# One down product for the whole sequence, with a second split in four of its seven products and operand sums made by transfers

## The chip, the cores and the metric

The kernel runs on one core of a Trainium2 chip. The metric is the device time in microseconds (us) of one execution. A core has five engines that run side by side: TensorE (PE) for matmuls, VectorE (DVE) and ScalarE (ACT) for element work, GpSimd (POOL), and SyncE (SP), which here only starts transfers. Each has its own queue of instructions and works through it in order. Sixteen DMA engines carry the transfers of all queues. Matmuls read operands from the on-chip memory SBUF and write to PSUM, eight banks of 128x512 floats each.

## The reference

One decoder layer on x of 2048 positions and 1024 channels, then a last norm: a mixing part (four HGRN2 heads, eight sliding-window attention heads, an output projection) and a gated MLP with a causal depthwise convolution. What matters here is the MLP:

```python
    v = rmsnorm(h, norm_ffn_w[l])
    gate = causal_depthwise_conv(v @ w_gate[l], conv_w[l], conv_b[l])
    h = h + (jax.nn.silu(gate) * (v @ w_up[l])) @ w_down[l]
return rmsnorm(h, final_norm_w)
```

`w_gate` and `w_up` are 1024 x 2816, `w_down` is 2816 x 1024, all float32.

## The kernel before

All activations stand transposed, channels on partitions. The sequence is done in two halves of 1024 positions (`hf` = 0, 1). For each half: the mixing part, the output projection (`out_proj`), the gate and up products (`gate_up`), the down product (`down`). A float32 operand is cut into a high part (`h`, a cast by ACT to the float32r format) and a low part (`l`, the difference, by DVE), and each product of tiles is three matmuls: high x high, high x low, low x high.

The three MLP products use the Winograd form of Strassen's scheme: with both operands split 2 x 2, seven products P1 to P7 stand for eight. In `down` the splits are the 22 k-tiles of 128 channels (even and odd, 11 each), the 8 output tiles (4 and 4) and the 1024 positions (lo and hi, 512 each). The activation operands `B11, T1, B21, T2, T3, B22, T4` are computed by DVE at the end of each pair of `gate_up` and stored to DRAM (`acts`, L1092 to L1105). The weight operands are the four quadrants `A11` to `A22` of `w_down` and the sums `S1` to `S4`, which DVE makes inside `down` (`w_op`, L1125 to L1141). `prep_piece` loads and cuts two k-tiles at a time, two pieces ahead. A product has 4 output tiles, 11 k-tiles and 3 terms: 132 matmuls of 128x512; seven products and two halves make 1848. Sums in PSUM run on from product to product (`bx` on four banks of the pool `mm`, `by` on the banks `hg` and `at`).

`down` of the first half also loads, cuts and sums the squares of the second half's x (`load`, from three pieces before P4 on), so that the key and value units (`first_unit`) and the unit `f` of the second half can follow at once. In the last half the final norm runs beside the last product P4, done column by column (`column`), the last two of them in halves of 256 positions.

`gate_up` goes through 11 pairs of output tiles. Each pair has a gate unit and an up unit (`pair_unit`) of 7 x 12 = 84 matmuls, 1848 in a half. Its weights come through the ring `raw` of three tiles, and its activation operands T2, T3, B22 and T4 lie in the pool `x`, which holds the tiles of x in the mixing part.

The order of instructions on each engine is fixed when the program is built, by a planner that models the time of each instruction and takes from each engine's queue what it expects to be ready first. Instructions of several jobs are put between each other. `tc.issue_after` pins an order. SP issues nearly all transfers, ACT a few small ones; POOL issues none.

Of the kernel before, what the change touches and what calls it, by code (L numbers as in the profile page):

```python
# [17 lines left out]
P = 128  # L18
# [13 lines left out]
PIECES = [2, 2, 2, 2, 2, 1]  # L32
OPS = ["B11", "T1", "B21", "T2", "T3", "B22", "T4"]
QUADS = ["A11", "A12", "A21", "A22"]
PRODUCTS = [("P1", "A11", "B11"), ("P5", "S1", "T1"), ("P6", "S2", "T2"), ("P3", "S4", "B22"),
            ("P7", "S3", "T3"), ("P2", "A12", "B21"), ("P4", "A22", "T4")]
# [17 lines left out]
def hymba_layer(ctx: ExitStack, tc: tile.TileContext, a: dict, out: bass.AP):  # L54
# [8 lines left out]
    xp = pool("x")  # L63
    wp = pool("w")
    hp = pool("h")
    sp = pool("small", bufs=2)
    sp.tile([P, 48], F32, name="pad", bufs=1)
    dp = pool("dram", space=bass.MemoryType.DRAM)
# [758 lines left out]
    def out_proj(hf, M, p):  # L827
# [6 lines left out]
        ops = Operands(p)  # L834
        ops.get("B11", 0)
        kept, v = {}, {}
# [4 lines left out]
        for d, part in parts:  # L841
# [18 lines left out]
            k = kept[d] = dp.tile([P, HALF], F32, name=f"keep{hf}{d}")  # L860
# [3 lines left out]
            for b, bs in halves():  # L864
# [8 lines left out]
                nc.sync.dma_start(k[:, bs], t[:, bs])  # L873
# [36 lines left out]
        return kept, ops, st, first, leftovers  # L910
# [48 lines left out]
    def pair_unit(W, ops, p, evac, then={}, behind_first=None):  # L959
# [35 lines left out]
        if behind_first:  # L995
# [13 lines left out]
            return  # L1009
        prod(X, "S2", "T2", True)  # L1010
        u2 = out(X, "u2")
        Y = ps("hg", "Y")
        prod(Y, "S1", "T1")
        s5 = out(Y, "s5")
# [8 lines left out]
    def gate_up(hf, ops, hs, nxt, last, p):  # L1023

        acts = {op: [dp.tile([P, n, 512], F32, name=f"act{hf}{op}{i}") for i, n in enumerate(PIECES)] for op in OPS}
# [7 lines left out]
        for pr in range(FT // 2):  # L1033
# [21 lines left out]
            if pr == 0:  # L1055
# [5 lines left out]
                pair_unit(W, ops, p, gate, then, behind_first)  # L1061
# [5 lines left out]
            for i in range(2):  # L1067
# [9 lines left out]
                nc.vector.tensor_tensor(y, y, invb, op=ALU.mult)  # L1077
# [12 lines left out]
            pair_unit(W, ops, p, up)  # L1090

            y1, y2 = ys  # L1092
            dst = {op: acts[op][pr // 2][:, pr % 2] for op in OPS}
            tt = slot("T13")
            nc.sync.dma_start(dst["B11"], y1[:, lo])
            nc.sync.dma_start(dst["B21"], y2[:, lo])
            nc.sync.dma_start(dst["B22"], y2[:, hi])
            nc.vector.tensor_tensor(tt[:, lo], y1[:, hi], y1[:, lo], op=ALU.subtract)
            nc.sync.dma_start(dst["T1"], tt[:, lo])
            nc.vector.tensor_tensor(tt[:, hi], y2[:, hi], y1[:, hi], op=ALU.subtract)  # L1100
            nc.sync.dma_start(dst["T3"], tt[:, hi])
            nc.vector.tensor_tensor(y1[:, lo], tt[:, hi], y1[:, lo], op=ALU.add)
            nc.sync.dma_start(dst["T2"], y1[:, lo])
            nc.vector.tensor_tensor(y2[:, lo], y2[:, lo], y1[:, lo], op=ALU.subtract)
            nc.sync.dma_start(dst["T4"], y2[:, lo])  # L1105
        return acts

    def down(hf, kept, acts, p):
# [4 lines left out]
        lo, hi = slice(0, 512), slice(512, HALF)  # L1113
        final = hf + 1 == NH
        NP = len(PIECES)
        def ring(name, dt=F32):
            return p.tile([P, 512], dt, tag="ut", name=name, bufs=UT)

        todo = [(name, w, t, j) for name, w, t in PRODUCTS for j in range(NP)]
        S = {}  # L1120

        def w_raw(q, j, home=(p, "xl2", 6)):
            pl, tag, n = home
            t = pl.tile([P, PIECES[j], 512], F32, tag=tag, name="wr", bufs=n)
            nc.sync.dma_start(t, a["w_down"][QUADS.index(q), :, 2 * j:2 * j + PIECES[j]])  # L1125
            return t

        def w_op(w, j):
            if w == "S1":
                r1, r2 = w_raw("A21", j), w_raw("A22", j)  # L1130
                t = S[j] = p.tile([P, PIECES[j], 512], F32, tag="xh2", name="S", bufs=6)
                nc.vector.tensor_tensor(t, r1, r2, op=ALU.add)
            elif w == "S2":
                t = S[j]
                nc.vector.tensor_tensor(t, t, w_raw("A11", j), op=ALU.subtract)
            elif w == "S4":
                t = S[j]
# [43 lines left out]
        def done(st, d, bs):  # L1181
            st.add(hh[d][:, bs])
            weigh(d, bs)
# [202 lines left out]
```

## Time and profile before

| | us |
|---|---|
| median of three runs | 2114.2 |
| lowest and highest of them | 2114.07, 2114.67 |
| span of the profiled execution, first to last instruction | 2112.5 |

The profiled execution has no time of its own beside its span; the three runs stand for it. Granted clock of PE over the span: 0.999. Busy shares of the DMA engines in 40 equal slices of 52.8 us, in tenths, and GB/s:

```profile
DMA  4111111513332325964641111214233233269643
GB/s 161 42 51 34 33 42 53 175 60 115 102 122 86 119 96 185 389 213 157 218 134 52 31 34 35 77 45 149 80 100 130 88 102 120 85 217 385 230 149 135
```

The first of these lines peaks in slices 17 and 37, where the two down products begin. The rest of the profile is shown where the prediction uses it. How to read it: a row of the stage view gives a window and the busy time of each engine in it; a row of the groups gives line, engine, operation, output and inputs, shapes, count, busy time in us and the mean of one in ns; a row of the waits gives who waited for whom, for how long in total, how often, and the longest.

### The profile page before, as it was taken

The page shows a single profiled execution, that of the slowest core. Times are in us where ns is not written, and L with a number is a line of the kernel's source. Part 1 is how long each engine was busy: PE and PEld are TensorE (multiplying, and loading weights), DVE is VectorE, ACT ScalarE, POOL GpSimd, SP SyncE. Part 2 cuts the span into 40 slices and gives each one's busy share as a digit, 9 for nine tenths or more (in the row PEclk, how much of TensorE's full clock was granted, in tenths as well). Part 3 has the DMA queues.
Part 4 walks back from the last instruction along what each step waited for, and adds up shares of the span by engine and source line. Part 5 has one row for each costly group of instructions (what it writes and reads, how often), then busy time and mean ns, then how long its engine had stood idle before and what let it go on. Part 6 is the DMA issues. An engine that isn't in the chain of part 4 may idle for free.

```text
span 2112.5 us, 29613 instructions
## 1 busy us (share of the span) xinstructions
PE 2098.0 (99%) x11480; PEld 1740.9 (82%) x11480; DVE 1624.3 (77%) x2355; ACT 1088.1 (52%) x1877; POOL 24.6 (1%) x52
## 2 busy tenths in 40 slices
PE   9999999999999999999999999999999999999998
PEld 7888888888888888888888888888888888888887
DVE  7457887898888878786773677868988788887766
ACT  6365565664444445345744566656544444444354
POOL 2000000000000000000000000000000000000000
PEclk9999999999999999999999999999999999999999
DMA  4111111513332325964641111214233233269643
GB/s 161 42 51 34 33 42 53 175 60 115 102 122 86 119 96 185 389 213 157 218 134 52 31 34 35 77 45 149 80 100 130 88 102 120 85 217 385 230 149 135
DMA packets 96617, 255.19 MB, mean 121 GB/s; under 512 B 17370, under 2 KB 19802, under 8 KB 96476
## 3 DMA queue, kind: packets, MB, share of 16 engines
q1 hardware_dynamic: 91220, 251.45, 34.9%
q10 hardware_dynamic: 5256, 1.85, 0.3%
q8 instruction: 90, 1.47, 0.3%
q14 instruction: 51, 0.42, 0.1%
HBM read 195.11 MB, written 57.16 MB: 119 GB/s over the span
## 4 chain that ended last, share of the span: by engine, by line
PE 96%; ACT 2%; DMA 1%; DVE 1%; issue 0%; SPq 0%; DVEq 0%
PE X L975 8%; PE X L976 8%; PE X L977 8%; PE pop L222 7%; PE hq L222 4%; PE q L222 4%; PE f L222 4%; PE pdx L1193 4%; PE pdx L1194 4%; PE pdx L1195 4%; PE Y L977 4%; PE Y L976 4%; PE Y L975 4%; PE g L222 3%; PE pdy L1194 3%; PE pdy L1193 3%
## 5 line engine op out<-in xcount | busy, mean ns | idle before, releaser
L800 ACT CAST whi<-raw 128x1024 fp32r<-128x1024 f32 x88 | 92.6, 1052 | 110.0 <-PE X L976 74.1
L975 PE MATMUL X<-T,whi 128*128 128x512 f32 x352 | 137.4, 390 | 0.0
L976 PE MATMUL X<-T,whi 128*128 128x512 f32 x352 | 137.0, 389 | 0.0
L977 PE MATMUL X<-T,wlo 128*128 128x512 f32 x352 | 137.0, 389 | 0.0
L1074 DVE SCALAR_TENSOR_TENSOR y<-ga,cw,y 128x1024 f32<-128x1024 f32 x88 | 112.3, 1278 | 25.7 <-ACT y L1072 25.7
L201 DVE TENSOR_TENSOR wlo<-raw,whi 128x1024 fp32r<-128x1024 f32 x57 | 69.3, 1218 | 60.8 <-ACT whi L200 60.5
L982 ACT COPY u<-X 128x512 f32<-128x512 f32 x88 | 51.6, 587 | 121.4 <-PE X L977 121.3
L801 DVE TENSOR_TENSOR wlo<-raw,whi 128x1024 fp32r<-128x1024 f32 x88 | 107.1, 1217 | 2.1 <-ACT whi L800 2.1
L200 ACT CAST whi<-raw 128x1024 fp32r<-128x1024 f32 x57 | 59.6, 1048 | 77.9 <-PE q L222 22.3
L222 PE MATMUL pop<-XL,whi 128*128 128x512 f32 x256 | 88.8, 391 | 0.0
L222 PE MATMUL pop<-XH,whi 128*128 128x512 f32 x256 | 88.0, 393 | 0.0
L222 PE MATMUL pop<-XH,wlo 128*128 128x512 f32 x256 | 87.1, 390 | 0.0
L801 DVE TENSOR_TENSOR xld<-raw,xhd 128x1024 fp32r<-128x1024 f32 x72 | 80.2, 1129 | 8.7 <-ACT xhd L800 8.6
L679 ACT COPY G<-QK 128x1024 f32<-128x1024 f32 x48 | 51.4, 1071 | 66.7 <-DVE QK L683 45.5
L800 ACT CAST xhd<-raw 128x1024 fp32r<-128x1024 f32 x72 | 68.9, 978 | 27.0 <-DMA raw<-act1B 6.0
L975 PEld LDWEIGHTS X<-T,whi 128*128 128x128 f32 x352 | 66.0, 188 | 15.1 <-ACT u L982 1.6
L977 PEld LDWEIGHTS X<-T,wlo 128*128 128x128 f32 x352 | 66.1, 188 | 13.8
L976 PEld LDWEIGHTS X<-T,whi 128*128 128x128 f32 x352 | 66.1, 188 | 13.7
L683 DVE TENSOR_TENSOR QK<-QK,f 128x1024 f32<-128x1024 f32 x56 | 68.5, 1223 | 11.3 <-ACT G L679 11.1
L1194 PE MATMUL pdx<-xld,hid 128*128 128x512 f32 x192 | 74.7, 389 | 0.0
L1193 PE MATMUL pdx<-xhd,hid 128*128 128x512 f32 x192 | 74.2, 390 | 0.0
L1195 PE MATMUL pdx<-xhd,lod 128*128 128x512 f32 x192 | 72.4, 389 | 0.0
(393 smaller groups left out, 6280.6 us busy)
## 6 DMA issues: line engine op xcount, KB each, us to landing
wr<-in_w_down SPq DMA_DIRECT2D x90, 512.0 KB
raw<-in_w_gate SPq DMA_DIRECT2D x44, 512.0 KB
raw<-in_w_up SPq DMA_DIRECT2D x44, 512.0 KB
raw<-act0T SPq DMA_DIRECT2D x20, 512.0 KB
raw<-act1T SPq DMA_DIRECT2D x20, 512.0 KB
act0B<-y SPq DMA_DIRECT2D x33, 256.0 KB
act1B<-y SPq DMA_DIRECT2D x33, 256.0 KB
raw<-in_w_out SPq DMA_DIRECT2D x16, 512.0 KB
```

The source lines that it names most:

```text
L201: nc.vector.tensor_tensor(lo, raw, hi.bitcast(F32), op=ALU.subtract)
L222: marks["unit"] = nc.tensor.matmul(o[b], w, x[:, bs], start=f, stop=l)
L683: done = nc.vector.tensor_tensor(own, own, Fv.rearrange("p b w -> p w b").unsqueeze(3).to_broadcast([P, 2, nb, m]), op=ALU.mult)
L800: return (nc.scalar.copy(h, src), (eng or nc.vector).tensor_tensor(l, src, h.bitcast(F32), op=ALU.subtract))
L801: (eng or nc.vector).tensor_tensor(l, src, h.bitcast(F32), op=ALU.subtract))
L975: nc.tensor.matmul(o, wh[:, ws], xh, start=i == 0 and not more, stop=False, skip_group_check=more)
L976: nc.tensor.matmul(o, wh[:, ws], xl, start=False, stop=False, skip_group_check=more)
L977: r = nc.tensor.matmul(o, wl[:, ws], xh, start=False, stop=i == 3, skip_group_check=more)
L1074: nc.vector.scalar_tensor_tensor(y, g[:, w:w + HALF], C.cw[:, ft, w:w + 1], y, op0=ALU.mult, op1=ALU.add)
L1193: nc.tensor.matmul(o, wh[:, i, c], ah[:, i, cols], start=f, stop=False, skip_group_check=more)
L1194: nc.tensor.matmul(o, wh[:, i, c], al[:, i, cols], start=False, stop=False, skip_group_check=more)
L1195: nc.tensor.matmul(o, wl[:, i, c], ah[:, i, cols], start=False, stop=l, skip_group_check=more)
```

## The change

`down` is no longer called for each half. The halves' activations are kept in DRAM, and one product for all 2048 positions follows the second half's `gate_up`. Each of the seven products now has 11 k-tiles, 4 output tiles and 2 x 512 positions (512 of each half). P1, P6, P5 and P7 (`TWICE`) are split again into seven: k into 5 and 5 tiles (`KG`), output tiles into 2 and 2 (`m`), positions by half; the eleventh k-tile (`REST`) is multiplied in the plain way and added in the same banks. P3, P2 and P4 stay plain (`once`).

The steps of a split product, in order, with the bank pair, the activation operand, the weight operand and a sign; V has only the eleventh k-tile, on X's banks:

```diff
+KG = 5
+REST = FT // 2 - 2 * KG
+PRODUCTS = [("P3", "S4", "B22", 1), ("P1", "A11", "B11", 1), ("P6", "S2", "T2", -1), ("P5", "S1", "T1", -1),
+            ("P2", "A12", "B21", 1), ("P7", "S3", "T3", 1), ("P4", "A22", "T4", -1)]
+TWICE = ("P1", "P6", "P5", "P7")
+STEPS = [("X", "t11", "w11", 1), ("Y", "t1", "s1", 1), ("X", "t2", "s2", -1), ("Y", "t22", "s4", 1),
+         ("X", "t3", "s3", 1), ("Z", "t21", "w12", -1), ("V", None, None, 1), ("W", "t4", "w22", 1)]
```

Steps 0, 1, 2 and 4 are copied from PSUM to a tile of the ring `R` by ACT (s1, s5, u2, u3). Steps 3, 5, 6 and 7 add the eleventh k-tile, and DVE adds the bank to such a copy; the result is one 256-channel, 512-position part, which `total` adds to the output tiles `H` (in SBUF, positions `hi`) and, for positions `lo`, to the residual kept in DRAM, by an accumulating transfer:

```diff
+            def total(m, hf, r):
+                for i in range(2):
+                    if name != "P7" or i == 1:
+                        add(H[hf, i, m], r)
+                    if name == "P1" or name != "P5" and i == 1:
+                        plus(kept[hf, i, 0, m], r)
...
+                    for e, o in enumerate(banks["X" if bank == "V" else bank]):
+                        if x:
+                            matmuls(o, whole(y), e * P, x, KG, first, not out)
+                        if out:
+                            key, m, hf = out
+                            rest(o, m, e, hf, ra, rw, False, True)
+                            nc.vector.tensor_tensor(keep[key][:, e], o, keep[key][:, e], op=ALU.add)
+                        else:
+                            nc.scalar.copy(keep[copy][:, e], o)
```

The second-level sums of the activations are made in DRAM, by transfers that POOL issues: plain copies, and transfers that add their source to what stands at the target. In the first half two of five k-tile pairs' parts are stored and copied; in the second half the rest follows. `combine` is called after each second pair of `gate_up`:

```diff
+    def plus(dst, src, **kw):
+        return nc.gpsimd.dma_start(dst, src, accum_op=ALU.add, **kw)
...
+        def store(self, hf, pr, src):
+            if pr >= 2 * KG:
+                nc.sync.dma_start(self.rest[hf][:, pr - 2 * KG], src)
+                return
+            k, g = divmod(pr, 2)
+            first, copy = f"t{g + 1}{hf + 1}", None
+            if self.twice:
+                first, copy = {(0, 0): ("t11", "t1"), (0, 1): ("t21", "t4"), (1, 0): ("t3", None),
+                               (1, 1): ("t22", "t2")}[hf, g]
+            t = self.t
+            nc.sync.dma_start(t[first][:, k], src)
+            if copy:
+                return nc.gpsimd.dma_start(t[copy][:, k], t[first][:, k])
+            if self.twice:
+                return plus(t["t1"][:, k], t["t3"][:, k])
...
+                plus(t["t3"][:, k], t["t22"][:, k])
+                plus(t["t2"][:, k], t["t1"][:, k])
+                plus(t["t4"][:, k], t["t2"][:, k])
```

All weight sums are made in the same way: `down_quads` copies the quadrants of `w_down` to DRAM tiles in the first half, four of the eight parts negated on the way (SP loads a chunk to the ring `raw`, ACT negates it, SP stores it), and `down_sums` makes S1 to S4 and the second-level sums, one sum at a time, four in the last pairs of the first half's `gate_up` and twenty in the first seven pairs of the second's:

```diff
+        for name, x, y in (("S1", "A21", "A22"), ("S2", "A11", "S1"), ("S3", "A11", "A21"), ("S4", "A12", "S2")):
+            for m in range(2):
+                t = N[name, m] = dp.tile([P, FT // 2, 256], F32, name=f"{name}{m}")
+                nc.gpsimd.dma_start(t, N[x, m])
+                for c in (slice(0, 8), slice(8, 11)):
+                    plus(t[:, c], N[y, m][:, c])
+                yield
...
+                t[name] = dp.tile([P, KG, 256], F32, name=f"{w}{name}")
+                nc.gpsimd.dma_start(t[name], t[x])
+                plus(t[name], t[y], max_dma_last_dim=KG * 1024)
+                yield
```

An operand is loaded three jobs ahead and cut two jobs ahead; 2560 columns for an activation, 1280 for a weight:

```diff
+        def prepare(n):
+            for t in jobs[n + 3][0] if n + 3 < len(jobs) else ():
+                t.fetch()
+            for t in jobs[n + 2][0] if n + 2 < len(jobs) else ():
+                t.cut()
```

The operands B11, T1 and B21 of `gate_up` move to a pool of their own on the right side of SBUF. It is closed (`leave`) in the last up unit before the product S2, with S1 moved ahead of S2 in that unit (`sooner`), and in the second half the first operands of the product are loaded and cut there. The other tiles of the product take the place of the pools `x`, `w` and `h`, which are closed (`layers.close()`). After the first half, what `down` did for the next half's x stands behind the last up unit:

```diff
+            if pr == FT // 2 - 1 and hf + 1 < NH:
+                ahead = first_units(hf + 1, ring)
...
+        X = []
+        W = prep(a["w_att"][ATT_J])
+        stage = iter([lambda: raw4(None)] * 2 + [lambda: slot("x")] * (KT - 2))
+        for xs in load(hf, X, lambda: next(stage)()):
+            pass
+        kv = [unit(W, X, "kv", kind="aux", then={7: lambda: (xs.everywhere(ring, aux), xs.column())})]
+        kv.append(first_unit(X, 1))
+        f0 = unit(a["w_f"][0], X, "f")
```

Signs are folded in where they cost an instruction already: the product with `invb` in `gate_up` is a `scalar_tensor_tensor` with -1 for some pairs, and a cut takes a sign. The final norm of all four quarters of the output now runs beside P4 of the one product, which is done column by column for both halves; the last two columns keep their halves of 256 positions.

More of the change, by code (lines that the diff above doesn't have):

```diff
@@ L1021, in pair_unit, with gate_up @@
         evac(1, 0, X, None)
[L1023 to L1025 removed]
+    def gate_up(hf, ops, hs, nxt, last, p, acts, quads, sums, leave):
         lo, hi = slice(0, 512), slice(512, HALF)
@@ new lines, in gate_up, with first_units @@
+            store("T4", y2[:, lo])
+            if pr % 2 == 1:
+                for op in acts:
+                    acts[op].combine(hf, pr // 2)
+            if hf == 0:
+                for _ in range(1 if pr < 6 else 2):
+                    next(quads, None)
+            with tc.issue_after(copied.ins) if pr < 2 * KG else ExitStack():
+                for _ in range(3 if hf else pr > 6):
+                    next(sums, None)
+        return ahead if hf + 1 < NH else None
+    def first_units(hf, ring):
+        X = []
[6 more added lines that the diff above has]
+        f0 = unit(a["w_f"][0], X, "f")
+        return X, kv, xs.acc, xs.rs, f0
@@ L1280, in down @@
-        f0 = unit(a["w_f"][0], X, "f")
-        return X, kv, xs.acc, xs.rs, f0
-    def finish(hf, hh, st, bs, queues, some=range(KT)):
-        for d in some:
-            t = hh[d][:, bs]
-            nc.vector.tensor_tensor(t, t, st.acc, op=ALU.mult)
-            queues[d % len(queues)].dma_start(out[d, :, hf * HALF + bs.start:hf * HALF + bs.stop], t)
+                finish(L, early, 1, 0, [nc.sync], c0, range(4, KT))
+            late.total(ring, "at", sq)
+            finish(L, late, 1, 0, [nc.scalar, nc.sync], c1)
@@ new lines, in down @@
+        pools["first"] = pool("first", side="right")
+        for t in jobs[0][0] + jobs[1][0][:1]:
+            t.cut()
+        pools["first"].tile([P, 56], F32, name="pad", bufs=1)
+        yield
+        pools.update({n: pool(n) for n in ("second", "third")})
+        for n in range(-2, len(jobs)):
+            prepare(n)
+            if n == 0:
+                for hf in range(NH):
+                    for i in range(2):
+                        for m in range(2):
+                            H[hf, i, m] = quarter(hf, i, 1, m, "hi")
+            if n >= 0:
+                jobs[n][1]()
@@ L1289, in hymba_layer @@
     X = []
     *nxt, summed = X, *head(X)
+    kept = {(hf, i, b, m): dp.tile([P, 2, 512], F32, name=f"keep{hf}{i}{b}{m}")
+            for hf in range(NH) for i in range(2) for b in range(NB) for m in range(2)}
+    acts = {op: Act(op, n in TWICE) for n, _, op, _ in PRODUCTS}
+    quads, sums = down_quads(), down_sums()
+    product = down(kept, acts)
     for hf in range(NH):
@@ L1321, in hymba_layer, with leave @@
             p = pool(f"ffn{hf}", stack=st, reuse_waits="tile")
-            kept, ops, hs, first, last = out_proj(hf, M, p)
-            acts = gate_up(hf, ops, hs, first, last, p)
-            nxt = down(hf, kept, acts, p)
+            early = ExitStack()
+            qp = pool("operands", stack=early, side="right")
+            def leave():
+                qp.tile([P, 56], F32, name="pad", bufs=1)
+                early.close()
+                if hf + 1 == NH:
+                    next(product)
+            ops, hs, first, last = out_proj(hf, M, p, kept, qp)
+            nxt = gate_up(hf, ops, hs, first, last, p, acts, quads, sums, leave)
+    layers.close()
+    next(product, None)
 def _layout(i):
```

446 lines of the change are left out of this document (266 added, 180 removed).

## The prediction

> **What bounds the kernel now.** I read the page's table of engines first, then the busy time by stage, then who waited for whom on TensorE (PE), then the chain of work that ended last.
>
> ```profile
> PE 2098.0 (99%) x11480; PEld 1740.9 (82%) x11480; DVE 1624.3 (77%) x2355; ACT 1088.1 (52%) x1877; POOL 24.6 (1%) x52
> ```
>
> PE is busy all the time. That alone says little, because matmuls overlap, so the next two views ask whether PE ever stands still. The stage rows hold: window, its length, then busy time and instructions of PE, weight loads, DVE, ACT and POOL, the granted clock, the share of the DMA engines, GB/s. The five windows are gate/up of the first half, its down product, the start of the next half, gate/up of the second half, and its down product.
>
> ```profile
> 424.10:843.40 419.30, 419.30 (x1848) 346.19 (x1847) 357.02 (x458) 198.41 (x289) 0.00 (x0) 1.00 0.33 110
> 843.40:1054.40 211.00, 211.00 (x933) 174.67 (x932) 157.63 (x167) 108.36 (x124) 0.00 (x0) 1.00 0.69 245
> 1054.40:1079.00 24.60, 24.60 (x104) 19.32 (x103) 18.76 (x29) 8.51 (x13) 0.00 (x0) 1.00 0.48 174
> 1471.30:1890.00 418.70, 418.70 (x1845) 345.62 (x1845) 356.25 (x457) 197.46 (x289) 0.00 (x0) 1.00 0.33 109
> 1890.00:2107.00 217.00, 214.29 (x1007) 179.50 (x1005) 155.61 (x185) 98.19 (x123) 0.00 (x0) 1.00 0.65 229
> ```
>
> The waits of PE over the whole span (engine and line, releaser: us in total, times, longest):
>
> ```profile
> PE psc L520 <- DVE sc L529: 2.6, 2, 1.3
> PE kv L420 <- ACT whi L363: 1.3, 1, 1.3
> PE idle L104 <- DVE ones L91: 1.1, 1, 1.1
> PE psum L308 <- DVE invb L256: 1.0, 1, 1.0
> PE psum L325 <- ACT fsq L262: 0.5, 1, 0.5
> ```
>
> None of these five waits stands in gate/up, in a down product, or at the change from the first half to the second. There the number of matmuls sets the time and nothing else does. The pace of a 128x512 matmul is read from the chain of work, in its longest unbroken stretch of one line:
>
> ```profile
> 366.66 57.36 PE pop L222 x253
> ```
>
> 57.36 / 253 = 0.2267 us each. Check: 1848 of them would take 419.0 us, and the first gate/up window has 419.3. So an edit is worth 0.2267 us for each matmul it removes, less whatever idle time it opens in a kernel that has almost none.
>
> **The change part by part.**
>
> *Matmuls removed.* Before, a product of one half is 11 k-tiles x 4 output tiles x 3 terms = 132 matmuls, 14 products, 1848 in all. After, seven products cover both halves. Three of them (P3, P2, P4) have 264 each, as before. The four in TWICE have 7 steps x 2 output tiles x 5 k-tiles x 3 terms = 210, and 4 x 2 x 3 = 24 for the eleventh k-tile, which is not split: 234. Removed: 4 x 30 = 120 matmuls, **-27.2 us**. Nothing beyond this can be gained: there is no PE wait to remove in these stages, and the tail after 2107 keeps its form (two columns in halves of 256, the same last totals). The floor is 2114.2 - 27.2 = 2087.0.
>
> *VectorE (DVE) and ScalarE (ACT) inside the product.* The durations by shape, from the first down window:
>
> ```profile
> L801 DVE TENSOR_TENSOR xld<-raw,xhd 128x1024 fp32r<-128x1024 f32 x23 | 27.8, 1217 | 1.6 <-ACT xhd L800 1.5
> L801 DVE TENSOR_TENSOR xld<-raw,xhd 128x512 fp32r<-128x512 f32 x5 | 3.4, 683 | 0.3 <-ACT xhd L800 0.3
> L237 DVE SCALAR_TENSOR_TENSOR XL<-x,nmw,XH 128x1024 fp32r<-128x1024 f32 x8 | 10.1, 1282 | 4.0 <-ACT XH L236 4.0
> L1179 DVE TENSOR_TENSOR h<-h,pdx 128x512 f32<-128x512 f32 x12 | 7.8, 681 | 6.5 <-PE pdx L1195 6.5
> L800 ACT CAST xhd<-raw 128x1024 fp32r<-128x1024 f32 x22 | 22.8, 1050 | 9.2 <-DMA raw<-act0B 6.0 <-DMA raw<-act0T 3.3
> L800 ACT CAST xhd<-raw 128x512 fp32r<-128x512 f32 x5 | 3.1, 616 | 0.9 <-DMA raw<-act0T 0.9
> ```
>
> From 512 to 1024 columns DVE goes from 683 to 1217 ns, 1.04 ns a column; ACT from 616 to 1050, 0.85 ns. By these slopes (estimates, as no such width is in the trace) the low part of an operand of 2560 columns takes 2.82 us on DVE and its cast 2.35 on ACT; one of 1280 columns takes 1.49 and 1.27. A step of a split product is 30 matmuls, 6.80 us of PE, and needs one of each: 4.31 us of DVE, 3.62 of ACT. Over a whole split product DVE has 7 x 4.31 = 30.2, the unsplit rests 2 x 0.68 + 2 x 0.42 = 2.2, eight reads of PSUM at 0.68 = 5.4, and in P1, P6 and P5 eight additions of 128x1024 at 1.22 = 9.7: 47.5 us beside 234 x 0.2267 = 53.0 us of PE, 90%. Gate/up runs at 357.0 / 419.3 = 85% of DVE with no wait of PE, so 90% with operands cut two jobs ahead should nearly hold; P3, P2 and P4 have 59.9 us of PE and, for operands and sums, 25 of DVE. If the cover went, each of the 28 steps could wait for its own cut, 4.31 us at worst. Bounds: 0 to 28 x 4.31 = 121 us; I take **+4**, near the gate/up row.
>
> *Banks.* Step W takes the two PSUM banks that step V leaves, and V is only 6 matmuls, 1.36 us. DVE reads each bank in 0.68 us after V; W's first matmul can be late by one such read, four times a kernel: 0 (another job's matmuls put in between) to 4 x 2.4 = 10 us (two additions of 128x1024 ahead of the read). **+2.**
>
> *From the first half to the second.* The down product that covered the loads, cuts and square sums of the next half's x is gone; `first_units` stands behind the last up unit. Its eight x tiles take the slots of operands T2, T3, B22, T4 of that unit, the last two only after its last product. DVE owes 8 x 1.28 for the low parts (the row of L237) and 8 x 1.22 for the squares, 20.0 us, beside 144 matmuls = 32.6 us of the units kv, kv, f, which can start on the first six tiles. Bounds: 0 to 20.0, all of it in the open; **+2**.
>
> *Start of the product.* When `leave` runs, three up products of the last unit are out and four are ahead: 48 x 0.2267 = 10.9 us. In it the first operands have to come (1.31 + 0.66 MB) and be cut. The rate of the DMA engines when they are full, from 853 to 880 us, where the old product begins:
>
> ```profile
> DMA packets 3647, 11.27 MB, mean 417 GB/s; under 512 B 406, under 2 KB 406, under 8 KB 3646
> ```
>
> And one small transfer, from its issue on the ACT queue to the DVE instruction that waited for it:
>
> ```profile
> 1372.74 0.64 ACTq L647 DMA_DIRECT2D odd<-moved  x1
> 1374.82 0.31 DVE L654 COPY_PREDICATED strip<-lmask,odd 126x64 f32<-126x64 uint32 x1 [2.36 <-DMA odd<-moved]
> ```
>
> So 2.1 us of latency, 1.97 MB / 417 = 4.7, cast 2.35, low part 2.82: 12.0, 1.1 us late; 5.8 late if POOL's transfers hold half the engines; 12 if nothing is fetched before the unit ends. Bounds 0 to 12, **+4**.
>
> *Sums by accumulating transfers.* They leave DVE (the old S1, S2, S4, S3 sums) for POOL's queue, where no compute engine waits for them until P1, which comes after P3's 59.9 us. Weights: eight tiles of 1.44 MB and sixteen of 0.66 MB, each one copy and one accumulation, 22.0 MB of both; all but 5.8 MB of each falls in the second gate/up. Activations there: 20 copies and 80 accumulations of 0.262 MB. Second gate/up in all: 21.5 MB copied, 37.2 MB accumulated. The trace has no accumulating transfer. Lower bound: the price of a plain one, 37.2 / 417 = 89 us. Since it must read its target as well, I take two passes, 178 us, and as the upper end four, 357. With 0.33 x 418.7 = 138 us there now and 52 for the copies, the engines are taken for 138 + 52 + 178 = 368 of 418.7 us. It fits: **0**. The tiles `kept` get 16 accumulations of 0.52 MB inside the product, 40 us of engines at two passes, beside 84 MB of operands (8.7 MB for each of P3, P2, P4, 14.6 for each split product), 202 us, in 392 us of PE: 0, with P1 the tight place (its eight fall in the 53 us where 35 us of operands come in). In the first half the quads' negation adds 12 ACT passes and 12 uses of the raw ring, beside 198 us of ACT in 419: 0.
>
> The Trainium skill, Collectives: The Full Stack, in the section on the bandwidth ceiling, says that an add inside the DMA engines reads two sources on one ring and so runs at half the rate of a copy. By it the accumulations take 178 us where a plain transfer's row would give 89, and both fit the window; what it changes is the weight of the first rival below, which needs more than three passes. No run here shows it.
>
> *The sum.* -27.2 + 4 + 2 + 2 + 4 = -15.2 us. The profiled span is 2112.5; the median of the three runs is 2114.2, 1.7 us around it that the change doesn't touch. **2114.2 - 15.2 = 2099.0 us.**
>
> **The rivals.**
>
> *Late sums: slower.* POOL's queue is served in order, and each sum waits for its own copy. If an accumulation costs more than I take, the sums aren't ready when P1 fetches them, and PE stands. P3 hides 59.9 us, of which its own operands and the residual tiles need some 31 of the engines. So the lateness begins where 138 + 52 + a = 418.7 + 29, a = 258 us, 2.9 passes, and the gain is eaten at a = 285, 3.2 passes. At four passes: 357 - 258 = 99 late, 2099 + 99 = 2198. For it: 144 transfers in one queue, most behind another, with some 2 us of latency each (the odd<-moved row) are 300 us even before any bytes. Against: at two passes 51 us of the engines are still free, and P3 stands ahead. 0.19.
>
> *The split steps are too short: no gain.* If each of the 28 steps waits 1 us (a late cut, a bank, an operand behind `kept`'s accumulations), 28 us stand where I took 6: 2121. For: DVE at 90%, above any stage of today; against: the gate/up row at 85% without a wait. 0.18; by how long the wait is, 2108 to 2135.
>
> *Nothing opens up: 2087*, the floor. For it: matmuls of other jobs fill the gaps today. 0.08.
>
> **How the numbers follow.** The forecast (2088 to 2108) has 0.55. This kernel's runs lie within 0.03%, and 0.2% (4.2 us) is about what a measurement can tell from no change: 2110 to 2118.4. Faster: 0.55 + 0.08 and 0.03 of the second rival, 0.66. Same: 0.07 of the second rival. Slower: its other 0.08 and the late sums, 0.27. The range runs from the floor to 2130: it holds the forecast, most of the second rival and the mild end of the first, and leaves out the rest of the late sums.
>
> **What would show it.** Right: 120 fewer 128x512 matmuls, a pace of 0.2267 us, a product of about 1728 x 0.2267 = 392 us, and PE waits in it that add up to some 10 us, named after the cuts and banks. The PE row of the first gate/up stays near 419 us. Wrong: a PE or ACT wait that ends on a transfer from POOL's queue at the start of P1 (first rival; its length is the lateness), waits of about 1 us in step with the seven steps (second), or gate/up longer than 419 us because weight loads stand behind POOL's transfers, which I cost at nothing.

## The result, and the profile after

The changed kernel takes **2127.5 us** (median; 2122.4 to 2135.4), the kernel before 2114.2. The ratio is 1.0066, 95% interval 1.0043 to 1.0089: slower by 0.7%, where 2099.0 and faster was forecast. The range held the time; the sign was wrong. One run below, the profiled one of e8 (2146.4 us), is in a slower state of the chip and is left out of that row's ratio.

The execution that was profiled took 2135.4 us, with a span of 2133.7; it is the slowest of four, so its stages add up to 8 us more than the median. The page of the changed kernel: engines, busy tenths of the DMA engines in 40 slices, POOL's queue.

```profile
PE 2089.2 (98%) x11360; PEld 1725.6 (81%) x11360; DVE 1604.7 (75%) x2276; ACT 1112.3 (52%) x1862; POOL 175.6 (8%) x264
...
DMA  7111111434444589411112134999999686995584
...
q0 software_dynamic: 25920, 89.14, 18.6%
```

11480 - 11360 = 120 matmuls are gone, as worked out. New are q0 (POOL's queue, 89 MB) and a run of nines in slices 26 to 31, in the second gate/up; in that of before (slices 29 to 35) the digits are 2 and 3. The stages of the changed kernel (columns as in the prediction): first half from its first gate matmul to the next head's queries, mixing part of the second half, its gate/up, the product.

```profile
423.70:887.60 463.90, 458.43 (x2002) 375.67 (x2000) 385.92 (x493) 229.38 (x323) 30.09 (x52) 1.00 0.56 179
887.60:1268.90 381.30, 380.00 (x2777) 317.89 (x2776) 267.14 (x492) 222.36 (x501) 7.60 (x12) 1.00 0.19 61
1268.90:1720.00 451.10, 430.69 (x1848) 350.16 (x1847) 356.54 (x458) 196.60 (x286) 106.94 (x144) 0.98 0.88 228
1720.00:2121.00 401.00, 398.26 (x1807) 331.05 (x1807) 286.71 (x261) 209.90 (x211) 13.90 (x16) 1.00 0.74 261
```

The third row is the one to look at. In the second gate/up of before 1845 matmuls took 418.7 us; here 1848 take 451.1, and PE is busy for 430.7 of them. The product, which held most of my costs, has PE standing for 2.7 of 401.0.

Next, the DMA view of that stage in the changed kernel (busy tenths in 40 slices of 11.3 us, then packets, MB and share of the 16 engines by queue):

```profile
DMA  0131699999999999999999999999999989318999
...
q0 software_dynamic: 19072, 58.73, 60.2%
q1 hardware_dynamic: 16797, 43.98, 27.3%
```

In four slices at the start the engines are nearly idle, because no sum can start before the first pair is stored. Then they are at 0.9 or more for 27 slices, some 305 us. The gap behind them (slices 35 and 36) shows that the queue had been worked off but for the last pair's sums; POOL issues the last of those at 1704 us, and the product's first matmul stands at 1717. The share of 0.88 hid this: it is some 0.1 at the start and 1.0 for most of the rest. The stretch from 1350 to 1670 us in steps of 40 us (three of eight rows; the first seven have a DMA share of 1.01 to 1.05, the last 0.66):

```profile
1350.00:1390.00 40.00, 35.66 (x141) 27.50 (x140) 28.66 (x37) 15.70 (x24) 10.30 (x15) 0.91 1.04 283
1390.00:1430.00 40.00, 40.00 (x178) 33.13 (x177) 33.17 (x44) 17.06 (x25) 10.62 (x13) 1.00 1.05 264
...
1550.00:1590.00 40.00, 36.28 (x153) 29.17 (x152) 27.87 (x37) 15.18 (x21) 12.27 (x16) 0.96 1.04 253
```

All eight hold 1313 matmuls; at 0.2267 us these are 297.7 us, so 22.3 of 320 are lost. PE stands for 15.6 of them, in five of the steps; the rest falls in the three of these five where the granted clock is 0.91 or 0.96.

Who made PE wait? The waits of PE in that stage go to ACT (`Sh`, `s`, `u`: some 4 to 5 us each in total), which says little, so one looks further down, at what the engines feeding PE waited for:

```profile
DVE S L936 <- DMA raw<-in_w_up: 26.5, 7, 6.3
...
DVE y L1118 <- DMA B21t<-y: 22.0, 8, 6.3
...
PE Y L977 <- ACT Sh L804: 5.0, 4, 2.2
```

DVE waits for weight loads of SP's, and for SP's stores of activations that still read the slot it wants to write. The chain of waits has the same transfers (start, length):

```profile
1380.10 10.87 DMA raw<-in_w_gate
...
1402.19 17.91 DMA T3t<-T
...
1437.56 17.06 DMA T3t<-T
...
1484.43 9.39 DMA B21t<-y
1522.11 10.86 DMA B21t<-y
1561.32 15.13 DMA B21t<-y
```

The stores are of 256 KB, 0.6 us at the 417 GB/s of the prediction. The five on this chain take 9 to 18 from issue to release. SP's transfers are late here, and PE waits behind them; whether the sums make them late is for the experiments.

### The profile page after: what moved, and what is told of

Its sections match the earlier page's. It is cut to its first block, busy times and chain, and to the rows that moved or that the text cites. A ratio compares the mean times of both kernels' runs of the same rounds, so it can differ in the third digit from the quotient of the medians.

```text
span 2133.7 us, 29435 instructions
## 1 busy us (share of the span) xinstructions
PE 2089.2 (98%) x11360; PEld 1725.6 (81%) x11360; DVE 1604.7 (75%) x2276; ACT 1112.3 (52%) x1862; POOL 175.6 (8%) x264
## 5 line engine op out<-in xcount | busy, mean ns | idle before, releaser
L1255 DVE TENSOR_TENSOR al<-al,ah 128x2560 fp32r<-128x2560 f32 x34 | 96.0, 2824 | 79.8 <-ACT ah L1254 79.8
L977 PE MATMUL X<-T,whi 128*128 128x512 f32 x352 | 140.1, 398 | 4.6 <-ACT u L984 4.6
L978 PE MATMUL X<-T,whi 128*128 128x512 f32 x352 | 139.1, 395 | 0.0
L1254 ACT CAST ah<-al 128x2560 fp32r<-128x2560 f32 x34 | 79.6, 2342 | 89.9 <-DMA al<-B11t 30.2
L1300 PE MATMUL pd<-ah,wh 128*128 128x512 f32 (+1 forms) x260 | 97.4, 375 | 4.8 <-ACT wh L1254 4.8
L204 ACT CAST whi<-raw 128x1024 fp32r<-128x1024 f32 x57 | 59.6, 1048 | 74.8 <-PE q L226 22.3
L1301 PE MATMUL pd<-al,wh 128*128 128x512 f32 (+1 forms) x260 | 96.6, 373 | 0.0
L1302 PE MATMUL pd<-ah,wl 128*128 128x512 f32 (+1 forms) x260 | 96.4, 373 | 0.0
L977 PEld LDWEIGHTS X<-T,whi 128*128 128x128 f32 x352 | 67.4, 192 | 21.5 <-ACT u L984 7.7
L804 ACT CAST Sh<-S 128x1024 fp32r<-128x1024 f32 (+1 forms) x46 | 46.7, 1016 | 73.1 <-DVE S L937 71.4
```

Source lines behind the costliest of these rows:

```text
L804: return (nc.scalar.copy(h, src), (eng or nc.vector).tensor_tensor(l, src, h.bitcast(F32), op=ALU.subtract))
L977: nc.tensor.matmul(o, wh[:, ws], xh, start=i == 0 and not more, stop=False, skip_group_check=more)
L978: nc.tensor.matmul(o, wh[:, ws], xl, start=False, stop=False, skip_group_check=more)
L1254: nc.scalar.copy(h, raw)
L1255: nc.vector.tensor_tensor(l, raw, h.bitcast(F32), op=ALU.subtract)
L1300: nc.tensor.matmul(o, wh, xh, start=f and k == 0, stop=False, skip_group_check=True)
```

## The experiments

Theories. **A**: the sums' transfers crowd SP's loads and stores. **A1**: because POOL's rows are long (11, 8 and 5 KB for the weights), and SP's transfers wait until an engine is through with one. **A2**: because the engines have more to do in the stage than it has time for. **B** (rival): the sums cost little and the loss comes from the new product, the quads, or the change from half to half. **C** (rival): `kept`'s accumulations.

| kernel | median us (range) | ratio to before, 95% | first half | mixing 2 | gate/up 2 and product |
|---|---|---|---|---|---|
| changed | 2127.5 (2122.4-2135.4) | 1.0066, 1.0043-1.0089 | 463.9 | 381.3 | 851.9 |
| e1_early_wsums | 2160.9 (2158.6-2162.2) | 1.0219, 1.0204-1.0235 | 512.6 | 383.3 | 827.4 |
| e2_no_asums | 2128.3 (2123.4-2129.8) | 1.0062, 1.0047-1.0077 | 483.0 | 381.3 | 823.8 |
| e3_no_wsums | 2100.8 (2099.4-2101.9) | 0.9936, 0.9921-0.9951 | 454.7 | 381.6 | 824.4 |
| e4_no_sums | 2097.8 (2095.9-2099.2) | 0.9923, 0.9907-0.9940 | 454.7 | 381.4 | 822.3 |
| e5_rows4k | 2115.2 (2110.3-2121.1) | 1.0004, 0.9995-1.0014 | 466.4 | 381.4 | 829.2 |
| e6_in_mix | 2126.2 (2123.4-2128.8) | 1.0053, 1.0037-1.0068 | 454.7 | 405.1 | 828.7 |
| e7_spread2 | 2130.3 (2129.0-2134.7) | 1.0076, 1.0060-1.0092 | 464.5 | 381.5 | 849.5 |
| e8_no_kept_sums | 2127.7 (2113.5-2146.4) | 1.0058, 1.0021-1.0096 | 464.4 | 381.4 | 856.5 |
| e9_rows2k | 2112.3 (2106.8-2116.5) | 0.9988, 0.9979-0.9997 | 459.4 | 383.4 | 831.3 |
| e10_late | 2126.9 (2124.8-2130.5) | 1.0062, 1.0049-1.0074 | 454.8 | 380.9 | 852.4 |
| e11_rows4k_late | 2132.5 (2129.2-2136.1) | 1.0087, 1.0074-1.0101 | 454.7 | 381.3 | 860.7 |
| e12_rows2k_late | 2123.2 (2119.3-2124.5) | 1.0037, 1.0024-1.0051 | 454.7 | 381.4 | 848.1 |
| e13_in_mix_2k | 2122.5 (2121.7-2126.2) | 1.0042, 1.0029-1.0055 | 454.7 | 402.9 | 826.6 |
| e14_mix8_2k | 2102.6 (2100.9-2105.0) | 0.9945, 0.9931-0.9958 | 454.8 | 384.6 | 825.4 |
| e15_mix12_2k | 2110.7 (2105.1-2114.4) | 0.9982, 0.9973-0.9991 | 454.6 | 393.3 | 823.1 |
| e16_mix8 | 2105.4 (2104.1-2106.3) | 0.9955, 0.9941-0.9968 | 454.7 | 380.7 | 831.5 |

The last three columns are from the profiled execution of each: from the first gate matmul to the first query matmul of the next half's heads, from there to the first gate matmul of the second half, from there to the last column's last matmul. Before has 381.6 in the mixing part. All runs of one kernel are compared with runs of the kernel before from the same session (2114.2 to 2115.0).

**Which sums (e1 to e4).** First the sums were moved or left out. e1 hands out the weight sums in the second half's mixing part, without fixing their place in POOL's queue:

```diff
-                for _ in range(3 if hf else pr > 6):
+                for _ in range(0 if hf else pr > 6):
...
+                if hf and n % 2 == 0:
+                    next(sums, None)
```

> The twenty sums of the weights that POOL made in the second half's gate/up are issued in the second half's mixing part instead; nothing is left out. Theory (the DMA engines are full in the second gate/up, 397 of 451 us, and what SP loads and stores there lands late): about 133 us of transfers leave that stage, its DMA share falls from 0.88 to about 0.63, its length from 451 to 419-424 us, and the whole to 2100-2106 us (the 17 us lost elsewhere stay). Rival A (the new order of instructions or the weights' way through the raw ring costs the time, not the transfers): the stage stays above 440 us and the whole above 2118. Rival B (POOL's queue itself holds something up): the loss moves with the sums into the mixing part, which grows from 381 to over 400 us.

> The copies and accumulations of the activations are left out (the steps read t11, t21 and t22 in place of t1, t4 and t2, and t3 stays without its second term). Theory: 5.2 MB copied and 21 MB accumulated leave the second gate/up, its DMA share falls to 0.60-0.65 and its length to 419-425 us; the whole 2098-2106 us. If an accumulation costs what a copy does, the share falls only to about 0.74. Rival A: the stage stays above 440 us.

> All sums of the weights are left out (S1 to S4 and the second-level sums read one of their two terms). Theory: as the early sums, the second gate/up at 419-425 us, DMA share 0.60-0.65, the whole 2098-2106 us. From this share and that of the run without activation sums the price of a copied and of an accumulated MB follows: 16.25 MB copied and 16.25 MB accumulated are gone here, 5.2 and 21 there. Rival A: the stage stays above 440 us.

> Both are left out; the quadrants' copies in the first half and the accumulations into the kept residual in the product stay. Theory: DMA share of the second gate/up 0.33-0.36, its length 419-420 us, the whole 2094-2104 us, hardly below the two runs before, since either alone already empties the engines enough. Were it the number of transfers or bytes that counts in proportion, this run would gain twice what each of those two gains.

e1 and e2 missed their numbers. With the sums not fixed, the order written by the planner pulled weight sums forward into the first gate/up. There they made a loss that is larger still, 58 us in e1 and 28 in e2 over the 454.7 of a first half without weight sums: the DMA view of e1 from 424 us to the next head's queries.

```profile
DMA  1143749649318148148147149879999999999997
...
q0 software_dynamic: 9510, 46.26, 33.8%
```

The nines moved, and the loss with them: first half 512.6, second gate/up and product 827.4 (e2: 483.0 and 823.8). So a loss follows the weight sums to wherever they run, which speaks for A. e3 and e4 came as A said: without weight sums 2100.8, without any 2097.8. Beside no weight sums the activations' cost 3 us; the weights' cost 27 beside the activations'. The stages of e4, and the waits of PE in its product:

```profile
424.00:878.70 454.70, 454.70 (x2001) 375.25 (x2001) 386.09 (x492) 229.67 (x322) 0.00 (x0) 1.00 0.41 135
...
1260.10:1680.00 419.90, 417.52 (x1840) 344.76 (x1840) 354.63 (x455) 195.50 (x284) 0.00 (x0) 1.00 0.31 104
```

```profile
PE pd L1293 <- ACT wh L1247: 2.4, 1, 2.4
PE psum L327 <- DVE acc L260: 1.9, 1, 1.9
PE X L1293 <- ACT wh L1250: 1.3, 1, 1.3
PE X L1295 <- DVE wl L1251: 0.9, 1, 0.9
PE X L1294 <- DVE al L1248: 0.7, 1, 0.7
```

B falls: with quads, the new product and the changed boundary in place and only the sums gone, PE stands for some 5 us in the product (the psum wait is in the tail), and for nothing in the first half. DVE's waits of the second gate/up go too: 26.5 us for `raw<-in_w_up` and 22.0 behind `B21t<-y` in the changed kernel, none and 1.3 here. One thing is not held still: the planner orders the other engines anew when sums are left out. e5 and e9 below, with the order of the changed kernel on PE and SP, show that a new order isn't needed for a large part of the gain.

**How (e5 to e8).** The same bytes in shorter rows; the sums in the mixing part, fixed behind a clearing on POOL; two sums a pair in place of three in the second gate/up; and no `kept` accumulations.

```diff
-                nc.gpsimd.dma_start(t, N[x, m])
+                nc.gpsimd.dma_start(t, N[x, m], max_dma_last_dim=4096)
...
-                    plus(t[:, c], N[y, m][:, c])
+                    plus(t[:, c], N[y, m][:, c], max_dma_last_dim=4096)
```

> The weight sums' transfers are cut into rows of at most 4 KB (2.8, 2.5 and 4 KB) in place of 11, 5 and 8 KB; same bytes, and the order of instructions on PE, DVE, ACT and SP is the same row by row. Theory 1 (the engines are simply full for too long): nothing changes, the whole stays within 2120-2136 us and the second gate/up near 451 us. Theory 2 (a long row of an accumulation holds a DMA engine while SP's loads and stores wait their turn): SP's transfers land sooner, the second gate/up falls below 440 us and the whole below 2117.

> All 24 weight sums are issued in the second half's mixing part, six behind POOL's clearing of each head's tile, which POOL reaches only when that tile is free, so they can't run ahead into gate/up; nothing is left out. Theory (the sums cost time only where they meet gate/up's weight loads and stores): the way from the first gate/up to the next half's first hq unit falls from 464 to 454-456 us, the way from the second gate/up to the last column from 852 to 823-827, the mixing part stays at 381-386, the whole 2096-2104 us. Rival (any stage with 60% of the engines taken loses as much): the mixing part grows by 20 us or more, the whole 2115-2125.

> In the second gate/up two sums follow each pair (three the first) in place of three in the first seven pairs. If what counts is that the engines are full without a break for 300 us, the breaks give back 8-20 us (2107-2120). If it is the engine time in all (397 us of 451 taken), the loss stays: 2120-2132 us.

> The accumulations into the kept residual in the product are left out. The profile of the change shows one PE stand in the product, at about 1865 us, behind a load of T2's operand that took 19.3 us to land while they ran. Theory: that stand goes, 3-7 us off the product (2117-2129, measured against the change's 2127). If P1 is not held by them, no difference. The second gate/up stays at about 450 us.

e5 bears A1 out in part: same bytes, the same order on PE and SP, and 12 us less. The traces show what the rows do to an engine: in the changed kernel's second gate/up the copies of the large weight sums go as packets of 45 KB, 1.9 us of one engine each (128 of them); in e5 none of POOL's there is over 5 KB, and by size their means are 0.26 us at most. e7 gives nothing in all, but its trace says where: 19.7 us are lost from 1350 to 1510 us, in the pairs that begin with the large sums, and none in the 200 us after, with two small sums a pair. e8's runs spread over 33 us and the profiled one is the slowest of them, so it settles nothing on C. e6 missed: the second gate/up is cured (828.7), but the mixing part grew by 24 us. Its chain of waits holds four small shifts on the ACT queue in that part:

```profile
949.96 12.47 DMA odd<-moved
...
1033.84 13.82 DMA odd<-moved
...
1106.17 10.23 DMA odd<-moved
...
1180.90 6.52 DMA odd<-moved
```

The prediction has the row of one such shift before: 2.1 us from issue to use. Beside the sums these four take 6 to 14. DVE waits for such shifts 48.0 us over the whole kernel, 14.0 before.

**Rows or engine time (e9 to e13).** Rows cut at 2 KB (and POOL's ring of descriptors doubled, a second change); the four sums of the first half moved into the second gate/up; both together; and short rows in the mixing part.

```diff
-                for _ in range(3 if hf else pr > 6):
+                for _ in range(3 if hf else 0):
```

> Same bytes, same sums in the same places, the same order of instructions on PE, DVE, ACT and SP as in the changed kernel; only the rows of the weight sums' transfers are cut at 2 KB (before this 11, 8 and 5 KB; 4 KB in e5_rows4k, which took 2115.2 us), and POOL's ring of descriptors is doubled so that they fit. If the length of POOL's rows is what makes SP's loads and stores late: another step down, 2105 to 2113 us, with the second half from its first gate matmul to the last column at 822 to 828 us (851.9 in the changed kernel, 829.2 at 4 KB). If only the bytes in the stage count: no further gain, 2114 to 2118 us. The first half's part from the first gate matmul to the next head's queries stays at 462 to 467 us by both, since it was no shorter at 4 KB.

> The four weight sums that stand in the first half (S1 and S2) move to the second half's gate/up, which then starts three sums to a pair from its first pair; rows as in the changed kernel. If those four are what cost the first half its 8 us: the first half's part falls from 463.9 to 454 to 456 us, and the second half grows by their price there (four of 24 sums cost some 28 us there together, so 4 to 6 us more): 2118 to 2128 us. If the quads, or the change from the first half to the second, cost those 8 us: the first half stays at 462 to 465 us and the time rises to 2130 to 2140 us.

> e10_late with the weight sums' rows cut at 4 KB. If the losses of the first half (sums beside the loads of the next half's x) and of the second (long rows) are separate and add: first half 454 to 456 us, second 830 to 836 us, in all 2104 to 2112 us, faster than the kernel before. If the four sums cost as much wherever they stand: 2113 to 2118 us.

> e10_late with the rows cut at 2 KB and the doubled ring. If row length and place are the two causes, this does all the work of the changed kernel at 2099 to 2107 us, within 10 us of the kernel without any weight sums (2100.8). If the bytes count: 2112 to 2118 us.

> e6_in_mix (all 24 weight sums in the second half's mixing part; 2126.2 us, of which that part lost 24 us, with small shifts on the ACT queue that took 10 to 14 us where 2 were usual) with rows of 2 KB and the doubled ring; instruction order on PE, DVE, ACT and SP as in e6. If small transfers wait behind long rows of POOL's: mixing part 383 to 392 us (405.1 in e6), in all 2104 to 2113 us. If a full set of engines delays them whatever the row length: 400 to 406 us, 2120 to 2127 us.

e9: 2112.3, little below e5, and its second half (831.3) is no shorter than e5's (829.2), so the gain over 4 KB isn't where it was expected. e10: the first half is free of loss (454.8), so those four sums were its 9 us. By the medians the move gains nothing (2126.9 beside 2127.5). The changed kernel's profiled run lies 8 us above its median, so its second half is likely some 8 us shorter in a median run, and the four sums cost in the second gate/up about what they cost in the first; no profile shows this. Then the theory of long rows broke: e11 and e12 should have been at 2099 to 2112 and came at 2132.5 and 2123.2. The same 228 us at the head of the second gate/up in e10, e11 and e12, one row from each:

```profile
1262.00:1490.00 228.00, 222.79 (x967) 181.19 (x966) 184.57 (x243) 104.15 (x155) 43.01 (x60) 0.99 0.85 233
```
```profile
1262.00:1490.00 228.00, 227.15 (x999) 186.74 (x999) 195.56 (x255) 110.54 (x164) 38.66 (x47) 1.00 0.81 218
```
```profile
1262.00:1490.00 228.00, 227.14 (x999) 186.88 (x999) 195.70 (x255) 111.02 (x165) 44.94 (x49) 1.00 0.84 225
```

With short rows PE does 32 matmuls more (7.3 us) in the same time, and POOL gets through 11 to 13 fewer instructions, though it has as many. So short rows turn the loss over: SP's transfers come in time for PE, with the engines just as full, and the sums fall behind. The bill comes in the product. From the first gate matmul to the product's first, e10 takes 448.9 us and e12 427.5; the product then takes 403.5 in e10 and 420.6 in e12. In e12 POOL still issues activations' sums there, a weight operand of P1 needs 23 us to come in, and PE stands (a line of time, one of the chain, one of PE's waits):

```profile
1764.98 0.81 POOL L1144 DMA_DIRECT2D T2t<-T2t  x1 [1.02 <-DMA T2t<-T2t]
```
```profile
1744.37 23.39 DMA wl<-A
```
```profile
PE X L1300 <- ACT wh L1254: 15.4, 1, 15.4
```

The sums are late, as in the first rival of the prediction, but PE doesn't wait for one: this operand is a quadrant of the weights, which needs no sum, and its load is slow beside the late ones. It is the crowding again, one stage on. e13 fell too: 402.9 us of mixing with rows of 2 KB, 405.1 with the long ones. So shorter rows help in the gate/up and not in the mixing part, and they can't make up for too many sums. What is left to try is A2.

**Divided over two stages (e14 to e16).** Two weight sums to a head in the second half's mixing part, the eight large ones; two to a pair in its gate/up, the sixteen small ones. e15 puts three to a head; e16 is e14 with the changed kernel's rows and ring.

```diff
+            cleared = nc.gpsimd.memset(ST[i:i + 32, :, 0:i], 0.0)
+        if hf:
+            with tc.issue_after(cleared.ins):
+                for _ in range(2):
+                    next(wsums, None)
...
-                for _ in range(3 if hf else pr > 6):
+                for _ in range(2 if hf else 0):
```

> The eight large weight sums (S1 to S4, 23 MB moved) in the second half's mixing part, two to a head, the sixteen small ones (21 MB) in its gate/up, two to a pair; rows of 2 KB. If what is lost is engine time beyond what a stage has free, spreading it leaves both stages short of full: mixing part 383 to 390 us, from the second gate to the last column 823 to 829 us, 2099 to 2108 us in all. If sums cost alike wherever they stand, 2112 to 2123 us as in e9_rows2k and e12_rows2k_late.

> As e14_mix8_2k with three sums to a head (S1 to S4 and four small ones, 28 MB) in the mixing part and twelve small ones in the gate/up. Engine time beyond what is free: within 3 us of e14_mix8_2k. A price per byte in the mixing part, as e6 has it (24 us for 44 MB): 3 us above it there, and 1 to 4 less in the gate/up.

> The placement of e14_mix8_2k (2102.6 us) with the rows and the ring of the changed kernel (11, 8 and 5 KB); instruction order on PE, DVE, ACT and SP as in e14. If it is enough that no stage's engines are full: within 3 us of e14, 2100 to 2106 us. If long rows cost by themselves wherever they run: 2108 to 2118 us.

e14 does all the work of the changed kernel in **2102.6 us**, ratio 0.9945 (0.9931 to 0.9958): the best of all that leave nothing out, 12 us below before and 5 above the kernel without sums. Its first half, mixing part and second gate/up:

```profile
425.51:880.29 454.78, 454.78 (x2002) 375.19 (x2000) 386.36 (x493) 229.85 (x323) 21.26 (x40) 1.00 0.48 158
880.29:1264.90 384.61, 381.54 (x2777) 319.09 (x2776) 267.22 (x492) 222.46 (x501) 33.44 (x36) 1.00 0.45 120
1264.90:1716.00 451.10, 447.26 (x1963) 368.95 (x1962) 376.78 (x473) 211.21 (x296) 108.32 (x132) 1.00 0.84 220
```

451 us of second half now hold 1963 matmuls; in the changed kernel 1848. Over the whole kernel the MB moved are the same (353.5). The engines are not idle in between: of the ten 40-us steps of its second gate/up, four have a DMA share of 1.02 to 1.09, each followed by one of 0.97 or less, and PE stands for 0.01 us in all ten. e16 has the place alone: 2105.4, 22 us of the 25 between 2127.5 and 2102.6, with 3 left for the rows. Taken in the other order the rows alone (e9) give 15 and the place 10 more, so the two don't add: in the second gate/up and product each by itself does nearly the same, 829.2 to 831.3 us by rows (e5, e9) and 831.5 by place (e16), from 851.9. The place gives the first half too, 454.7 us where e5 and e9 have 466.4 and 459.4. What e16 takes out of the gate/up are the large sums, those with the packets of 45 KB; whether it gains there by their bytes or by their rows, no run separates. e15 missed (2110.7): its mixing part lost 12 us for 28 MB where e14 lost 3 for 23, e16 none for 23 and e13 21 for 44. The price there is not one per byte from the first on: the first 23 MB are nearly free, the next cost. That they fit between two uses of the small shifts is a possible reason, and was not tried by itself.

## Why the prediction was wrong

**The step that failed** is "the engines are taken for 138 + 52 + 178 = 368 of 418.7 us. It fits: **0**", with its last clause on who waits. Two things are wrong in it.

First the size. POOL's queue took 60.2% of 451 us = 271.5 where I had 52 + 178 = 230. The prices come from e3, which has the activations' transfers only: 40 copies in the first half (454.7 us), and the second gate/up (429 us, 20 copies and 80 accumulations), a row from each view of the queues.

```profile
q0 software_dynamic: 3200, 10.49, 7.4%
```
```profile
q0 software_dynamic: 13120, 26.22, 35.8%
```

7.4% of 454.7 is 33.6 us for 10.49 MB: a copy from DRAM to DRAM goes at 311 GB/s, where I had taken the 417 of loads into SBUF. 35.8% of 429 is 153.6; less 20 copies (16.8) it is 136.8 us for 20.97 MB: 153 GB/s, 2.7 passes of a load and not two. The Trainium skill (Collectives: The Full Stack, the section on the bandwidth ceiling) says of ReduceScatter that its add needs two source reads on one ring and so gets half the rate of a copy; the factor here agrees, 311 / 153 = 2.03. My mistake was to put it on the rate of a load. By these two prices the 21.5 MB of copies and 37.2 MB of accumulations would make 312 us; the queue took 271.5. The weights' longer rows are cheaper: their accumulations in packets of 8 KB went at 206 GB/s in the changed kernel's trace.

Then, and worse, the question. With the right size the sum would have said the same: 138 + 271.5 = 409.5 of 418.7 us, it fits. I asked whether the sums would be late, over the whole stage as an average, and costed nothing for what queues beside them. With sums possible only from about 1320 us on, the engines are full for some 300 us; and beside these rows that costs long before a sum is late, as PE stands within microseconds behind SP's loads and stores, and behind POOL's sums only at P1. I had named this among the things that would show me wrong ("gate/up longer than 419 us because weight loads stand behind POOL's transfers, which I cost at nothing"), without giving it a price or a chance. By the medians of the changed kernel and of e4 it costs 2127.5 - 2097.8 = **29.7 us**. In the profiled executions it is 463.9 - 454.7 = 9.2 in the first half, where I had assumed nothing of the four sums there, and 851.9 - 822.3 = 29.6 in the second; these add up to more because the changed kernel's profiled run lies 8 us above its median. That the range held the time is luck: its upper part was there for the two rivals, and neither took place in the changed kernel.

**The other terms**, from e4, which has them all without the sums: 2097.8 - 2114.3 = -16.5 us (beside the runs of before of its own session), forecast -15.2. Its waits and its tail make -27.2 + 5.3 + 3.2 = -18.7; the other 2.2 us I can't place. The nearness to the forecast is in part luck: the terms of +12 came to 5.3, and the tail, put at nothing, took 3.2.
- 120 matmuls, -27.2: right. The first half's gate/up in e4 has no PE wait.
- Cutting the operands on DVE, +4, banks, +2, start of the product, +4: together +10. Measured 5.3 us of PE waits, named after cuts (`wh`, `wl`, `al`); 3.7 of them are at `wh`, the cut of a step's weights. The widths behaved as extrapolated: 2.82 us forecast for the low part of 2560 columns, 2.824 measured; 2.35 for the cast, 2.342 measured.

```profile
L1255 DVE TENSOR_TENSOR al<-al,ah 128x2560 fp32r<-128x2560 f32 x34 | 96.0, 2824 | 79.8 <-ACT ah L1254 79.8
...
L1254 ACT CAST ah<-al 128x2560 fp32r<-128x2560 f32 x34 | 79.6, 2342 | 89.9 <-DMA al<-B11t 30.2
```

- From half to half, +2: not seen.
- "The tail keeps its form": no. From the last column's last matmul to the end it is 12.8 us in the changed kernel and in e4, 9.6 before, +3.2. In the chain of both, eight products of the final norm for the earlier 256 positions (L1421 in the changed kernel, 2.77 us) now stand between the last matmuls and the last positions' own norm. In the kernel before, half of these eight are done ahead of the last column's addition, and its chain has none.
- `kept`'s accumulations, 0, and the quads, 0: the quads cost nothing (454.7 without sums); of `kept` e8 says nothing certain, but e4 has them and PE waits 5.3 us in its product, which is the most that they can make PE wait there; in the changed kernel's product PE stands for 2.7.

**The rivals.** Late sums was wrong for the changed kernel; in e12 the sums are late, but what PE waits for there is a load beside them. Split steps too short: not seen. The 0.27 for slower stood on these two, so it was the wrong mechanism with the right sign: the crowding that took place had no chance of its own.

**How sure.** That the sums' transfers cause the loss is shown by e3 and e4. That the place of the sums makes most of the loss is shown by e14 and e16 (the same bytes and sums in other places, e16 with the same rows too). That rows decide who waits in the gate/up is shown by e5, e9 and e10 to e12. That the place counts because of the engines' time in a stage is argued: in e12 the engines are as full as in e10, and PE stands for 2.2 of the first 400 us of the gate/up where it stands for 15.1 in e10, so a full set of engines is not enough by itself. The Trainium skill (DMA: Bandwidth & Descriptors, the section on queues, rings and completion order) says that an engine goes round its rings and changes only between packets; that short rows give SP its turn sooner fits this, but no run here shows the engine's turns themselves. Open stay e11, 6 us above e10 with a PE wait of 14.3 us in its product and two of 5 to 6; why 23 MB are free in the mixing part and 28 are not; and what `kept` costs.

## What to carry to other kernels

Work that is moved from a compute engine to the DMA engines is paid in their time: price it by the kind of transfer (here 3.2 us a MB for a copy in DRAM and 6.5 for an accumulation in rows of 2 KB, against 2.4 for a load), lay it on the stretch in which it can run, and not on the stage's average. If that stretch comes out full, the transfers that a compute engine waits for within microseconds can be late long before the moved work itself is. Then try two things: divide the work over stages, and cut the rows of the background transfers. Here each by itself cured most of the loss of the second gate/up, and neither sufficed everywhere: short rows didn't help in the mixing part, nor where the stage had more sums than it could finish.

## What the runs showed of the hardware that was not expected

- By the time that their packets took on the 16 engines, accumulating transfers between DRAM tiles in rows of 2 KB went at 153 GB/s and plain copies at 311 (both e3); loads went at 417 (before).
- The copies of the large sums went as packets of 45 KB, 1.9 us of one engine each, in the changed kernel.
- Beside POOL's sums, stores of 256 KB from SP that stand on the chain took 9 to 18 us (changed kernel), and a small shift on the ACT queue up to 13.8 (e6), where one took 2.1 before.
- In three of the five 40-us steps in which PE stood for 2 to 4 us the granted clock was 0.91 or 0.96, so the stands went with a loss of more than their length: 22.3 us where PE stood for 15.6 (changed kernel).
